# Summing squares at a layer's end: all eight on the vector engines instead of six, with two left to TensorE

## The chip, the cores and the metric

The kernel runs on one NeuronCore of a Trainium2 chip. The core has a matrix engine (TensorE, PE in the profile, with its weight loads shown as PEld), three engines for elementwise work (VectorE = DVE, ScalarE = ACT, GpSimd = POOL) and a queue that issues its transfers (SyncE = SP). Each engine takes its instructions strictly in the order of its own queue, and engines wait for each other through semaphores. The metric is the device time of one execution in microseconds; lower is better.

## The reference, cut to what matters

The computation is a two-layer encoder in float32 over two independent sequences, a prompt of 256 tokens and a sample of 512 tokens, with a model width of 1024. Layer 0 mixes tokens with an mLSTM, layer 1 with sliding-window attention; each layer ends in a convolutional feed-forward block, and each block is entered through an RMS norm.

```python
def rmsnorm(x, g):
    xf = x.astype(jnp.float32)
    y = xf * lax.rsqrt(jnp.mean(xf * xf, axis=-1, keepdims=True) + EPS)
    return (y * g.astype(jnp.float32)).astype(x.dtype)

def trunk(x, c, ...):
    for l in range(DEPTH):                                   # DEPTH = 2
        sh1, sc1, g1, sh2, sc2, g2 = ...                     # modulation from c
        h = rmsnorm(x, norm_g[l, 0]) * (1 + sc1) + sh1
        y = mlstm_mixer(h, ...) if l % 2 == 0 else swa_mixer(h, ...)
        x = x + g1 * y
        h = rmsnorm(x, norm_g[l, 1]) * (1 + sc2) + sh2
        x = x + g2 * conv_ffn(h, ...)
    return rmsnorm(x, final_g)
```

What matters here is the norm that follows a layer's feed-forward block: after layer 0 it is the norm in front of layer 1's attention, after layer 1 it is the final norm that makes the output. For each token it needs the mean of 1024 squares.

## The kernel before, in words

Activations are kept transposed: channels lie on the 128 partitions, in eight chunks of 128 channels (`KC` = 8), and tokens lie along the free axis, 768 of them (prompt first, then sample). The mean over channels is therefore a sum over eight chunks and over 128 partitions. Products of the large matrices are done as three TensorE passes over a high and a low half of each operand (`whi`, `wlo`), so one output tile of 128 channels by 256 tokens of the down projection takes six matmuls.

The feed-forward block (`ffn`) runs over eleven parts of the hidden width. In the last part, `down` handles the tokens in three ranges of 256: the two halves of the sample (here called range 0 and range 1) and the prompt. For each range it makes eight tiles, one per chunk. After each tile `resid` (line 590, DVE) adds it to the residual stream, and `Norm.square` squares the new chunk on ACT (line 111) and adds the square to a running sum (line 115) as long as the chunk's number is below `KC - on_pe`. Layer 0's adds run on GpSimd, layer 1's on VectorE.

After the eight tiles of a range its norm is queued as a generator (`stages`), whose steps are emitted between later tiles. The first step sums what is left over the partitions by matmuls with a constant vector of 1/1024 (`inv`): one matmul per summand and per block of 128 tokens, so two per summand here; in the trace each such float32 matmul leaves two records. Then come `+ EPS` (line 152), a power of -0.5 on GpSimd (line 153), and a matmul with the identity (`kct`) that spreads the result over the partitions. With it `apply` follows: after layer 0 `modulated` (lines 549 to 552), which writes the input `zh`, `zl` of the attention's projections; after layer 1 `output` (lines 574 to 582), which scales by the final gain on DVE (line 581) and GpSimd (line 579) and sends the result out.

The prompt's norm after layer 1 is the very last (`final`) and is handled apart: all of its squares go straight to TensorE (line 129). In `on_pe` terms: 8 for that one, 2 for the five others.

The order of instructions on each engine is set when the program is built, by a scheduler that works with its own estimates; only some stretches are written out by hand. Tiles for the results of matmuls (`pa`) come from a pool of four, temporary tiles (`nt`) from a pool of eight.

Of the kernel before, what the change touches and what calls it, by code (L numbers as in the profile page):

```python
# [18 lines left out]
KC = D // P  # L19
# [5 lines left out]
RANGES = ((256, 512, 0), (512, 768, 0), PROMPT)  # L25
# [54 lines left out]
def col(t):  # L80

    return t + (GAP if t >= 256 else 0)
# [85 lines left out]
class Net:  # L168
# [1203 lines left out]
    def ffn(self, l, xt, pool, last_tile, apply, keep=None):  # L1372
# [68 lines left out]
        def down(p, g):  # L1441
            ws = (w for _, w in self.halves(u0 + 3 * p + 2))
            chunk = lambda w, i: [t[:, 512 * i : 512 * (i + 1)] for t in w]

            def tile(w, c, rng):
                s0, s1, _ = rng
                o = self.pa()[:, : s1 - s0]
                cs = slice(c % 4 * P, (c % 4 + 1) * P)
                for i in range(2):
                    wh, wl = chunk(w, i)  # L1450
                    gh, gl = (g[:, z, i, col(s0) : col(s0) + s1 - s0] for z in range(2))
                    self.mm(o, wh[:, cs], gh, i == 0, False)
                    self.mm(o, wh[:, cs], gl, False, False)
                    self.mm(o, wl[:, cs], gh, False, i == 1)
                self.resid(xt, o, l, 40, c, rng)

            if p < NPART - 1:
                for h, w in enumerate(ws):
                    for rng in SAMPLE, PROMPT:
                        for c in range(4 * h, 4 * h + 4):  # L1460
                            tile(w, c, rng)
                return
            ws = list(ws)
            for rng in RANGES:
                final = keep is None and rng is RANGES[-1]
                norm = Norm(
                    self, xt, rng, apply, KC if final else 2, final,
                    None if keep is not None else nc.vector, 0.0 if keep is None or rng is RANGES[-1] else 1.3,
                )
                for c in range(KC):  # L1470
                    tile(ws[c // 4], c, rng)
                    norm.square(c)
                    if final and c > 1:
                        norm.begin(c - 1)
                    self.tick(0.65)
                if keep is not None:
                    self.save_x(xt, keep, rng)
                self.start(rng, norm.stages())

        prev = None  # L1480
        for p in range(NPART):
            g = up(p)
            if prev is not None:
                down(*prev)
            prev = (p, g)
        down(*prev)


# [179 lines left out]
```

## Time and profile before

| What | Before |
|---|---|
| Median of 3 runs | 1844.58 us |
| Lowest, highest | 1842.21 us, 1845.0 us |
| Profiled execution, its time | 1843.78 us |
| Its span, first to last instruction | 1842.0 us |
| TensorE busy | 1793.2 us, 97% of the span |
| VectorE, ScalarE, GpSimd busy | 1367.0, 895.3, 488.0 us |
| Mean granted TensorE clock | 0.994 |

A row of the timeline gives the start in us from the span's start, the length in us of what is merged in the row, the engine, the line, the operation, what it writes and reads, the size, how many instructions it stands for, and in brackets how long the engine sat idle before and what ended that. A length includes the emptying of a pipeline, so successive rows overlap; the time that an instruction takes from its engine is read from one start to the next. A row of windows gives a stretch, its length, the busy time of each engine in it with the number of instructions, then the granted TensorE clock (1.00 is full), and the share and rate of the transfers.

### The profile page before, as it was taken

How to read it: one execution, taken by the hardware profiler on the slowest of the kernel's cores; microseconds unless marked ns; L12 is line 12 of the kernel's file. 1: busy time of each engine (PE TensorE's matmuls, PEld its weight loads, DVE VectorE, ACT ScalarE, POOL GpSimd, SP SyncE). 2: the span in 40 equal slices, each digit the busy share in tenths (PEclk: the TensorE clock that was granted, in tenths of full speed). 3: DMA queues.
4: the chain of work that ended last, by engine and by line, in shares of the span. 5: the costliest groups of instructions: out<-in, count | busy, mean ns of one | idle time of the engine just before them, and what ended most of it. 6: DMA issues, size and time to landing. Idle time of an engine off the chain costs nothing.

```text
span 1842.0 us, 28931 instructions
## 1 busy us (share of the span) xinstructions
PE 1793.2 (97%) x11290; PEld 1657.4 (90%) x11290; DVE 1367.0 (74%) x2101; ACT 895.3 (49%) x1815; POOL 488.0 (26%) x386
## 2 busy tenths in 40 slices
PE   6999999999999999999999999999999999999997
PEld 3987887889998999999999999889989999999997
DVE  4755676886689877777777757766898777777776
ACT  4443443354456444444444556765564444444443
POOL 1001001021024333333331313430144333333322
PEclk9999999999999999999999999999999999999999
DMA  8344566546312221222223321124122222222212
GB/s 330 119 145 134 172 195 221 164 138 219 101 46 74 76 61 66 69 69 69 69 69 93 104 83 50 53 94 129 50 86 69 69 69 69 69 69 70 69 35 69
DMA packets 64245, 184.48 MB, mean 100 GB/s; under 512 B 6167, under 2 KB 23831, under 8 KB 64108
## 3 DMA queue, kind: packets, MB, share of 16 engines
q1 hardware_dynamic: 64108, 182.63, 30.8%
q8 instruction: 89, 1.46, 0.3%
q14 instruction: 48, 0.39, 0.1%
HBM read 176.17 MB, written 6.43 MB: 99 GB/s over the span
## 4 chain that ended last, share of the span: by engine, by line
PE 86%; DVE 6%; DMA 3%; ACT 2%; issue 1%; POOL 1%; SPq 0%; POOLq 0%; ACTq 0%; DVEq 0%
PE ps L254 27%; PE pa L254 25%; PE ps L1169 10%; PE ps L1172 10%; PE ps L1170 10%; PE pa L1008 1%; DMA slab<-in_adaln_w_dram 1%; DMA raw<-in_w_dram 1%; DVE wlo L261 1%; DVE ada L506 1%; DVE slab L590 1%; DMA raw<-in_adaln_w_dram 0%; PE pa L1172 0%; PE pa L1169 0%; PE pa L1170 0%
## 5 line engine op out<-in xcount | busy, mean ns | idle before, releaser
L260 ACT CAST whi<-raw 128x1024 fp32r<-128x1024 f32 x237 | 247.9, 1048 | 350.4 <-PE pa L254 161.4
L261 DVE TENSOR_TENSOR wlo<-raw,whi 128x1024 fp32r<-128x1024 f32 x237 | 316.6, 1337 | 119.8 <-ACT whi L260 117.3
L254 PE MATMUL pa<-slab,whi 128*128 128x256 f32 (+1 forms) x1472 | 346.6, 331 | 3.2 <-DVE slab L590 3.2
L254 PEld LDWEIGHTS pa<-slab,whi 128*128 128x128 f32 x1472 | 252.7, 188 | 27.5 <-DVE slab L590 4.5
L590 DVE SCALAR_TENSOR_TENSOR slab<-pa,mod,slab 128x256 f32<-128x256 f32 (+1 forms) x368 | 211.2, 592 | 70.8 <-PE pa L254 70.5
L254 PE MATMUL pa<-slab,wlo 128*128 128x256 f32 (+1 forms) x736 | 233.9, 330 | 0.0
L254 PE MATMUL ps<-zh,whi 128*128 128x256 f32 (+1 forms) x560 | 189.0, 339 | 2.3 <-ACT whi L260 1.7
L254 PE MATMUL ps<-zh,wlo 128*128 128x256 f32 (+1 forms) x560 | 184.1, 330 | 2.0 <-DVE wlo L261 2.0
L254 PE MATMUL ps<-zl,whi 128*128 128x256 f32 (+1 forms) x560 | 185.1, 332 | 0.0
L1169 PE MATMUL ps<-zh,whi 128*128 128x384 f32 x504 | 172.3, 342 | 3.6 <-ACT nt L1240 1.8
L1170 PE MATMUL ps<-zl,whi 128*128 128x384 f32 x504 | 169.9, 337 | 0.8 <-DVE zl L1126 0.8
L1172 PE MATMUL ps<-zh,wlo 128*128 128x384 f32 x504 | 168.9, 335 | 0.0
L254 PEld LDWEIGHTS pa<-slab,wlo 128*128 128x128 f32 x736 | 138.5, 188 | 13.1 <-DVE wlo L261 0.4
L1205 POOL TENSOR_TENSOR raw<-raw,raw 128x512 f32<-128x512 f32 x40 | 52.2, 1305 | 330.8 <-DVE wlo L261 259.4
L254 PE MATMUL ps<-slab,whi 128*128 128x384 f32 x512 | 132.0, 339 | 0.9 <-DVE slab L261 0.5
L1402 POOL TENSOR_TENSOR slab<-slab 128x772 f32<-128x772 f32 x44 | 86.5, 1967 | 164.6 <-DVE slab L1390 152.7
L1389 DVE SCALAR_TENSOR_TENSOR slab<-slab,cstt,slab 128x771 f32<-128x771 f32 x88 | 103.6, 1179 | 26.6 <-ACT slab L1387 26.5
L254 PEld LDWEIGHTS ps<-zh,whi 128*128 128x128 f32 x560 | 107.4, 192 | 15.9 <-issue 4.4
L506 DVE SCALAR_TENSOR_TENSOR ada<-raw,silc,ada 128x1024 f32<-128x1024 f32 x84 | 110.6, 1354 | 14.9 <-DMA raw<-in_adaln_w_dram 14.8
L1202 POOL TENSOR_TENSOR raw<-raw 128x512 f32<-128x512 f32 x40 | 68.5, 1712 | 200.1 <-DMA raw<-in_w_dram 169.7
L254 PEld LDWEIGHTS ps<-zh,wlo 128*128 128x128 f32 x560 | 107.2, 192 | 12.2 <-DVE wlo L261 2.9
L254 PEld LDWEIGHTS ps<-zl,whi 128*128 128x128 f32 x560 | 107.4, 192 | 11.9 <-issue 3.4
(291 smaller groups left out, 4265.7 us busy)
## 6 DMA issues: line engine op xcount, KB each, us to landing
raw<-in_w_dram SPq DMA_DIRECT2D x208, 512.0 KB, 3.7
raw<-in_adaln_w_dram SPq DMA_DIRECT2D x84, 512.0 KB, 4.6
slab<-in_x_dram SPq DMA_DIRECT2D x12, 512.0 KB, 6.8
slab<-in_adaln_w_dram SPq DMA_DIRECT2D x12, 512.0 KB, 10.3
slab<-mrows SPq DMA_DIRECT2D x8, 384.0 KB, 5.3
xs<-slab SPq DMA_DIRECT2D x6, 512.0 KB, 3.6
bt<-brow SPq DMA_DIRECT2D x16, 192.0 KB, 3.0
slab<-xs SPq DMA_DIRECT2D x6, 512.0 KB, 6.9
```

Source lines behind the costliest of these rows:

```text
L254: self.nc.tensor.matmul(out, lhsT, rhs, start=start, stop=stop)
L260: nc.scalar.copy(hi, src)
L261: return nc.vector.tensor_tensor(lo, src, hi.bitcast(F32), ALU.subtract)
L506: stt(acc[:, s], row, w, acc[:, s], ALU.mult, ALU.add)
L590: self.nc.vector.scalar_tensor_tensor(x, o, self.mod[l][:, gc + c, q : q + 1], x, ALU.mult, ALU.add)
L1169: mm(o, wh[:, k], hi[k], start=start and k == 0, stop=False, skip_group_check=True)
L1170: mm(o, wh[:, k], lo[k], start=False, stop=False, skip_group_check=True)
L1172: mm(o, wl[:, k], hi[k], start=False, stop=k == 3, skip_group_check=True)
L1202: tt(q[2], q[2], q[3], ALU.add)
L1205: tt(q[0], q[2], q[0], ALU.subtract)
L1389: stt(y[:, 1:], u[:, :-1], w(0), y[:, 1:], ALU.mult, ALU.add)
L1402: nc.gpsimd.tensor_tensor(y, y, yrow[:, j], ALU.mult)
```

## The change

For the first two ranges at the end of each layer `on_pe` goes from 2 to 0. The condition in `square` then holds for all eight chunks, so the squares of chunks 6 and 7 are also added to the running sum (two more adds per range at line 115, on GpSimd in layer 0 and on VectorE in layer 1), and one summand is left for the matmuls with `inv` where there were three. The prompt's ranges keep what they had: 2 after layer 0, all 8 after layer 1.

```diff
             for rng in RANGES:
                 final = keep is None and rng is RANGES[-1]
                 norm = Norm(
-                    self, xt, rng, apply, KC if final else 2, final,
+                    self, xt, rng, apply, KC if final else 2 if rng is RANGES[-1] else 0, final,
                     None if keep is not None else nc.vector, 0.0 if keep is None or rng is RANGES[-1] else 1.3,
                 )
```

In the built program this takes 16 `inv` matmuls (32 records) away and adds four adds on GpSimd and four on VectorE. The order of the other instructions changes only around the two layer ends. The transfers are the same, in the same order.

## The prediction

> **What bounds the kernel now.** I read the page's busy times and its chain first, then the groups by shape, then the timeline of each engine over the two layer ends, and last windows of the granted clock.
>
> ```profile
> PE 1793.2 (97%) x11290; PEld 1657.4 (90%) x11290; DVE 1367.0 (74%) x2101; ACT 895.3 (49%) x1815; POOL 488.0 (26%) x386
> PE 86%; DVE 6%; DMA 3%; ACT 2%; issue 1%; POOL 1%; SPq 0%; POOLq 0%; ACTq 0%; DVEq 0%
> ```
>
> TensorE is busy for 97% of the span and is 86% of the chain. Work taken from it is worth its full time, but only where no new wait opens in its queue; a wait that opens is paid in full as well.
>
> ```profile
> L254 PE MATMUL pa<-inv,nt 128*128 128x2 f32 x188 | 25.6, 259 | 1.1 <-DVE nt L115 0.6 <-ACT nt L111 0.3 <-POOL nt L115 0.3
> L115 POOL TENSOR_TENSOR nt<-nt,nt 128x256 f32<-128x256 f32 x25 | 19.2, 769 | 29.6 <-ACT nt L111 28.2
> ```
>
> The first row holds all matmuls with `inv` but the final norm's, 188 records. The change removes 32 of them. Its 259 ns is a length with an overlapping tail, so I price by starts below.
>
> **The change part by part.** Layer 0's end, TensorE first, then GpSimd, then ScalarE:
>
> ```profile
> 1021.74 0.40 PE L254 MATMUL pa<-slab,whi 128*128 128x256 f32 x2
> 1021.97 0.28 PE L254 MATMUL pa<-slab,wlo 128*128 128x256 f32 x1
> 1022.51 1.50 PE L254 MATMUL pa<-inv,nt 128*128 128x2 f32 x12 [0.26 <-POOL nt L115]
> 1023.87 0.48 PE L254 MATMUL pa<-slab,whi 128*128 128x256 f32 x2
> ...
> 1033.88 0.95 PE L254 MATMUL pa<-inv,nt 128*128 128x2 f32 x8
> 1034.68 0.36 PE L254 MATMUL ps<-zl,whi 128*128 128x256 f32 x1
> ...
> 1035.12 0.40 PE L254 MATMUL pa<-slab,whi 128*128 128x256 f32 x2
> ```
> ```profile
> 1018.44 4.02 POOL L115 TENSOR_TENSOR nt<-nt,nt 128x256 f32<-128x256 f32 x5 [9.37 <-ACT nt L111]
> 1023.36 0.73 POOL L115 TENSOR_TENSOR nt<-nt,nt 128x256 f32<-128x256 f32 x1 [0.91 <-ACT nt L111]
> ```
> ```profile
> 1021.39 0.42 ACT L111 ACTIVATE nt<-slab 128x256 f32<-128x256 f32 x1 [0.29 <-DVE slab L590]
> ...
> 1022.87 0.42 ACT L111 ACTIVATE nt<-slab 128x256 f32<-128x256 f32 x1 [0.29 <-DVE slab L590]
> ...
> 1032.79 0.81 ACT L111 ACTIVATE nt<-slab 128x256 f32<-128x256 f32 x2 [0.34 <-DVE zl L552]
> ```
>
> *Saved on TensorE.* Eight records cost 1034.68 - 1033.88 = 0.80 us and twelve cost 1.36, so 0.10 to 0.11 each. Eight records fewer in each of four ranges are 32 x 0.10 to 0.11 = 3.2 to 3.6 us; with the upsets of the matmul behind each scattered group, some 4 us at most.
>
> *Range 0 of layer 0, +1.5.* The five adds start 1018.44 and end 1022.46, (4.02 - 0.74)/4 = 0.82 from one to the next, and TensorE already waits for the fifth: it starts `inv` at 1022.51, 0.05 later. The changed program leaves the group at the same place of TensorE's queue, behind range 1's second tile, which ends about 1022.09. On GpSimd the order becomes: chunk 6's add, range 1's first add, chunk 7's add. Chunk 6's add runs 1022.54 to 1023.28. Range 1's add cannot start before its square, the row at 1022.87, ends at 1023.29; it starts at 1023.36 as now and ends 1024.09. Chunk 7's add is queued behind it, though its square (1021.39) is long there, and runs 1024.13 to 1024.87. TensorE starts `inv` at 1024.92 and needs 0.44 for four records (price quoted below, 1821.86 to 1822.30), so it is free at 1025.36 where it was at 1023.87: +1.49. The empty stretch is 1022.09 to 1024.92, 2.8 us. Behind the waiting group stand range 1's other tiles; DVE's residual adds and range 0's power wait for them, so everything shifts alike. If GpSimd put chunk 7's add ahead, the shift would be 0.8; if the extra adds were hidden it would be -0.9. I take +1.5, from the rows' own times.
>
> *Range 1 of layer 0, +0.1.* Eight records go (-0.8); a prompt tile moves from ahead of the group to behind it, and the three projection matmuls now behind it (1034.68 to 1035.12) move ahead. The square of chunk 7 is the first of the two at 1032.79 and ends near 1033.20; its add would then end at 1034.0 and `inv` start at 1034.05, take 0.44, upset the next matmul by 0.09, and the moved tile costs 0.70: 1035.28 (before the shift of +1.5). Now the same work is done at 1035.12. I call it +0.1, between -0.8 (add hidden) and +0.3.
>
> Layer 1's end, TensorE, then DVE, then ScalarE:
>
> ```profile
> 1812.10 0.39 PE L254 MATMUL pa<-slab,whi 128*128 128x256 f32 x2
> 1812.45 0.28 PE L254 MATMUL pa<-inv,nt 128*128 128x2 f32 x2
> ...
> 1817.00 0.71 PE L254 MATMUL pa<-kct,nr 128*128 128x128 f32 x4 [0.22 <-POOL nr L153]
> 1817.46 0.48 PE L254 MATMUL pa<-slab,whi 128*128 128x256 f32 x2
> ...
> 1821.86 0.58 PE L254 MATMUL pa<-inv,nt 128*128 128x2 f32 x4 [0.62 <-DVE nt L115]
> 1822.30 0.48 PE L254 MATMUL pa<-slab,whi 128*128 128x256 f32 x2
> ...
> 1823.81 0.95 PE L254 MATMUL pa<-inv,nt 128*128 128x2 f32 x8
> 1824.62 0.59 PE L129 MATMUL pa<-inv,nt 128*128 128x2 f32 x4
> ```
> ```profile
> 1812.08 1.06 DVE L590 SCALAR_TENSOR_TENSOR slab<-pa,mod,slab 128x256 f32<-128x256 f32 x2
> ...
> 1818.15 1.66 DVE L581 SCALAR_TENSOR_TENSOR slab<-slab,cstt,pa 128x256 f32<-128x256 f32 x4
> ...
> 1821.30 0.41 DVE L115 TENSOR_TENSOR nt<-nt,nt 128x256 f32<-128x256 f32 x1
> ```
> ```profile
> 1812.59 0.42 ACT L111 ACTIVATE nt<-slab 128x256 f32<-128x256 f32 x1 [0.18 <-DVE slab L590]
> ...
> 1817.75 0.37 ACT L574 COPY nt<-pa 128x256 f32<-128x256 f32 x1
> ```
>
> Half a tile is 1812.45 - 1812.10 = 0.35, a tile 0.70.
>
> *Range 0 of layer 1, +0.3.* Now TensorE spreads the group over the next four tiles, so nothing waits. In the changed order the whole group stands behind range 1's first tile, at 1812.45. DVE has the two residual adds until about 1813.06, then chunk 6's add; chunk 7's square ends at 1812.59 + 0.42 = 1813.01, and its add, which needs the one before, ends about 1813.81. From DVE to TensorE the row at 1821.30 gives 1821.86 - 1821.71 = 0.15. So `inv` runs 1813.96 to 1814.40, four tiles and an upset of 0.09 take 2.91, and the spreading matmul `kct` starts at 1817.31 instead of 1817.00. The new gap is 1.5 us; the 0.22 that `kct` waits now is gone.
>
> *Range 1 of layer 1, +1.0.* From `kct`, done at 1817.77, TensorE makes four tiles until 1820.68 and then stands before `inv`, which needs the sum of all eight. DVE is late: `output` of range 0 puts five multiplications of line 581, 0.39 apart ((1.66 - 0.48)/3), ahead of chunk 6's residual add. They wait for the copy of line 574, which stands behind chunk 4's square: tile until 1817.31, residual add from 1817.51 for 0.48, square 0.42, copy 0.37, so 1818.86 with the steps between engines. They also stand behind chunk 5's residual add (tile until 1818.56, add from 1818.76, 0.40) and the add of chunk 4 (0.33), so they run 1819.49 to 1821.45. Behind them come three residual adds (0.40 each) and three adds of squares (0.33, or 0.41 when the next one needs it): 1823.81. `inv` runs 1823.96 to 1824.40, two prompt tiles follow until 1825.90. Now the same work is done at 1824.62: +1.28 for both ranges of this layer. The gap is 3.3 us; the waits of 0.62 here and one before it vanish. If DVE kept the multiplications back, the gap would fall to some 1.3 us and the layer to -0.7.
>
> *Sum of waits and work:* 1.5 + 0.1 + 1.3 = +2.9. It is paid in full: from layer 0's end TensorE is the chain, and what is late next is only itself.
>
> *The clock.* Gaps of this length have a second price here:
>
> ```profile
> 121.70:125.11 3.41, 1.53 (x7) 0.83 (x6) 3.41 (x7) 1.12 (x2) 0.00 (x0) 1.00 0.77 262
> 125.12:128.53 3.41, 3.41 (x10) 2.64 (x9) 3.41 (x6) 0.00 (x0) 0.00 (x0) 0.50 0.85 293
> ```
> ```profile
> 145.60:149.01 3.41, 1.77 (x16) 1.53 (x14) 2.09 (x4) 1.49 (x6) 2.50 (x2) 1.00 0.02 5
> 149.02:152.43 3.41, 2.98 (x23) 2.78 (x24) 2.80 (x7) 2.62 (x10) 0.00 (x0) 1.00 0.26 87
> 1056.96:1060.37 3.41, 1.22 (x4) 0.31 (x4) 3.32 (x6) 3.38 (x11) 0.00 (x0) 1.00 0.00 0
> 1060.37:1063.78 3.41, 3.41 (x17) 3.41 (x17) 3.31 (x9) 2.02 (x5) 0.00 (x0) 0.50 0.22 54
> 1063.78:1067.19 3.41, 3.41 (x31) 3.41 (x30) 1.96 (x3) 0.92 (x1) 0.00 (x0) 1.00 0.41 133
> ```
>
> The halved stretches fall on a common grid of 3.41 us. Where TensorE was busy 1.22 or 1.53 us of a stretch, the next ran at clock 0.50; after 1.77 us it did not. So some 1.9 us empty within one stretch is enough. The halved stretch passed 17 matmuls where the next passed 31: 14 x 0.118 = 1.65 us lost, if TensorE sets the pace in it. The gap of 2.8 us holds 1.9 in one stretch for (0.9 + 0.9 + 0.6)/3.41 = 0.7 of the positions of the grid, that of 3.3 us for (1.4 + 1.4 + 0.1)/3.41 = 0.85; the gap of 1.5 us for none. Each drop costs between 0 (all of it in waits on DVE that are there anyway) and 1.65; near the upper end, since both gaps are followed by dense tiles: 1.5.
>
> The Trainium skill, "TensorE: Matmul & The Clock Gate", Part 1, says that the clock falls after at least one idle window of about 3.4 us, and tells to avoid gaps above that. By that sentence alone neither gap would drop the clock and the sum would stay at +2.9; this trace differs, since 1.22 us of work in a stretch did not keep the clock up. The same section's window of 3413 ns and its two rates agree with the 3.41 and 0.50 here.
>
> *Total:* 2.9 + 2 x 1.5 = +5.9, so 1843.78 + 5.9 = 1849.7 for the profiled execution. That one lies 0.8 below the median of the three runs; against the median it is 1844.58 + 5.9 = 1850.5.
>
> **The rivals.**
> - *One clock drop only,* because the grid cuts the other gap in two: 2.9 + 1.5, 1849.0.
> - *Waits, but no drop,* because a stretch of 3.41 must be empty from end to end, which no gap of 3.3 us or less can fill: 2.9 alone, 1847.5. For it: 1.77 us of work was enough at 145.60. Against it: the two halved stretches. This is the rule of the skill's page above.
> - *It is faster:* the extra adds end before TensorE arrives, and the 32 records are a clear gain of 3.2 to 4: 1840.9. The place is the first group of layer 0. It decides if chunk 7's sum is there by 1022.5 + 1.0, that is 1.4 us earlier than by GpSimd's rows, and if DVE in layer 1 is likewise 1.3 us earlier. TensorE already waits 0.26 and 0.62 for these very adds, which speaks against it.
> - *Worse:* range 1 of layer 0 gets the c7 sum late as well and a third drop follows: about +9, 1853.5. For it: TensorE waits for DVE's `zl` in that stretch; against it: DVE is busy there, not stalled.
>
> **How the numbers follow.** Two drops 0.47 (1850.5), one 0.27 (1849.0), none 0.13 (1847.5), faster 0.05 (1840.9), worse 0.08 (1853.5). The time is that of two drops; its own range is 1849 to 1852. The range 1846.5 to 1853.0 takes in one drop and none, with about 1 us for the spread of the runs (1842.21 to 1845.0), and leaves out the faster and most of the worse case. 0.2%, or 3.7 us, is about what a measurement of this kernel can tell from no change: 1848.3 is the limit. Slower: 0.47 + 0.08 + 0.8 x 0.27 = 0.77; same: 0.13 + 0.05 = 0.18; faster 0.05.
>
> **What would show it.** In the changed profile: 156 records of `inv` at line 254; a wait of TensorE for line 115 on GpSimd of 2.5 us or more near 1022, and two for line 115 on DVE, about 1.5 us near 1814 plus the shift and 3 us near 1822 plus the shift; clock 0.50 for 3.41 us just after the first and the last of these. I am wrong if the waits are below 1 us, which would mean that the added sums come earlier than the rows' pitches say, or if the clock stays up after gaps of 2.8 and 3.3 us.

## The result, and the profile after

The changed kernel takes 1856.70 us (median of 6 runs, 1852.19 to 1858.62) where the kernel before takes 1844.79 us in the runs beside it (median of 6): 1.0063 times as long, 95% interval 1.0052 to 1.0074, or +11.9 us. The direction was forecast, the size was not: 1850.5 with a range up to 1853.0. The profiled execution took 1855.8 us, 12.0 above that of before.

The page's busy times and chain, then two groups by shape (busy time in us, mean ns, idle time before and what ended it):

```profile
span 1853.8 us, 28886 instructions
...
PE 1796.3 (97%) x11258; PEld 1660.0 (90%) x11258; DVE 1367.6 (74%) x2105; ACT 894.7 (48%) x1815; POOL 493.3 (27%) x390
...
PE 86%; DVE 7%; DMA 3%; ACT 2%; issue 1%; POOL 1%; SPq 0%; POOLq 0%; DVEq 0%; ACTq 0%
```
```profile
L115 POOL TENSOR_TENSOR nt<-nt,nt 128x256 f32<-128x256 f32 x29 | 24.1, 832 | 29.9 <-ACT nt L111 28.5
L254 PE MATMUL pa<-inv,nt 128*128 128x2 f32 x156 | 22.5, 268 | 9.4 <-DVE nt L115 5.0 <-POOL nt L115 4.1 <-ACT nt L111 0.3
```

The 32 records of `inv` are gone, yet TensorE is busy 3.1 us longer (1796.3 for 1793.2): fewer instructions, some of them at half clock. And the matmuls with `inv` now have 9.4 us of idle time ahead of them where they had 1.1, nearly all of it for the adds of line 115. The four sums, in TensorE's timeline:

```profile
1024.01 0.61 PE L254 MATMUL pa<-inv,nt 128*128 128x2 f32 x4 [2.57 <-POOL nt L115]
...
1034.89 0.39 PE L254 MATMUL ps<-zl,whi 128*128 128x256 f32 x1 [0.56 <-DVE zl L552]
...
1037.84 0.61 PE L254 MATMUL pa<-inv,nt 128*128 128x2 f32 x4 [1.54 <-POOL nt L115]
...
1820.72 0.61 PE L254 MATMUL pa<-inv,nt 128*128 128x2 f32 x4 [1.44 <-DVE nt L115]
...
1831.11 0.98 PE L254 MATMUL pa<-inv,nt 128*128 128x2 f32 x4 [3.57 <-DVE nt L115]
```

Three of these waits are followed by a clock of 0.50. In the windows below, laid on the grid of 3.41 us that this execution shows, the clock is the number behind the five engines' busy times:

```profile
1021.96:1025.37 3.41, 1.35 (x11) 1.36 (x12) 0.17 (x2) 0.42 (x1) 2.34 (x4) 1.00 0.33 111
1025.38:1028.79 3.41, 3.41 (x18) 3.41 (x17) 1.45 (x3) 1.04 (x3) 1.69 (x3) 0.50 0.18 64
...
1035.62:1039.03 3.41, 1.87 (x16) 1.67 (x15) 2.62 (x7) 1.12 (x3) 3.27 (x4) 1.00 0.06 15
1039.04:1042.45 3.41, 3.41 (x18) 3.41 (x18) 1.46 (x4) 1.67 (x3) 0.88 (x2) 0.51 0.10 34
1042.45:1045.86 3.41, 3.41 (x31) 3.41 (x31) 3.28 (x6) 1.82 (x5) 3.17 (x4) 1.00 0.66 186
1827.51:1830.92 3.41, 0.03 (x1) 0.00 (x0) 3.31 (x9) 1.22 (x3) 0.41 (x1) 1.00 0.72 244
1830.93:1834.34 3.41, 3.23 (x15) 3.26 (x16) 0.68 (x3) 0.14 (x1) 0.69 (x1) 0.50 0.10 35
1834.34:1837.75 3.41, 3.41 (x18) 3.41 (x18) 0.97 (x2) 1.34 (x4) 0.00 (x0) 0.50 0.00 0
1837.76:1841.17 3.41, 3.41 (x32) 3.41 (x32) 2.24 (x6) 1.01 (x3) 1.42 (x2) 1.00 0.11 36
```

A halved stretch makes 18 matmuls where a full one makes 31 or 32 (the one at 1830.93 makes 15, because the wait still reaches into it). There is one behind each wait of layer 0, and two in a row behind the second wait of layer 1.

With the same matmuls of both traces laid side by side (all but those with `inv`, in order, start against start), the 12.0 us by which the profiled executions differ fall as follows:

| Where | Shift gained there |
|---|---|
| From the start to layer 0's end | -0.8 us |
| Layer 0's end | +6.3 us: wait of range 0 1.4, halved stretch 1.5, range 1 3.4 |
| Near 1343 us, inside layer 1 | +1.1 us |
| Layer 1's end | +5.0 us |

The rest, 0.4 us, lies behind the last matmul and in rounding. The +1.1 us is not at a sum at all. One VectorE subtraction of line 1126, which takes 0.55 us elsewhere, took 1.64 us because a GpSimd operation had started just ahead of it:

```profile
1341.95 2.31 DVE L1126 TENSOR_TENSOR zl<-slab,zh 128x384 fp32r<-128x384 f32 x2
```
```profile
1342.56 1.28 POOL L1205 TENSOR_TENSOR raw<-raw,raw 128x512 f32<-128x512 f32 x1 [22.88 <-DVE zl L1126]
```

### The profile page after: what moved, and what is told of

Same layout as the page of the kernel before. It is cut to its first block, busy times and chain, and to the rows that moved or that the text cites. A ratio compares the mean times of both kernels' runs of the same rounds, so it can differ in the third digit from the quotient of the medians.

```text
span 1853.8 us, 28886 instructions
## 1 busy us (share of the span) xinstructions
PE 1796.3 (97%) x11258; PEld 1660.0 (90%) x11258; DVE 1367.6 (74%) x2105; ACT 894.7 (48%) x1815; POOL 493.3 (27%) x390
## 3 DMA queue, kind: packets, MB, share of 16 engines
q8 instruction: 88, 1.44, 0.3%
## 4 chain that ended last, share of the span: by engine, by line
PE 86%; DVE 7%; DMA 3%; ACT 2%; issue 1%; POOL 1%; SPq 0%; POOLq 0%; DVEq 0%; ACTq 0%
PE ps L254 27%; PE pa L254 25%; PE ps L1169 10%; PE ps L1172 10%; PE ps L1170 10%; PE pa L1008 1%; DMA slab<-in_adaln_w_dram 1%; DMA raw<-in_w_dram 1%; DVE wlo L261 1%; DVE slab L590 1%; DVE ada L506 1%; DMA raw<-in_adaln_w_dram 0%; PE pa L1170 0%; PE pa L1172 0%; PE pa L1169 0%
## 5 line engine op out<-in xcount | busy, mean ns | idle before, releaser
L254 PE MATMUL pa<-slab,whi 128*128 128x256 f32 (+1 forms) x1472 | 350.6, 334 | 2.8 <-DVE slab L590 2.4
L254 PEld LDWEIGHTS pa<-slab,whi 128*128 128x128 f32 x1472 | 256.8, 192 | 26.9 <-DVE slab L590 3.6
L254 PEld LDWEIGHTS pa<-slab,wlo 128*128 128x128 f32 x736 | 140.9, 192 | 13.1 <-DVE wlo L261 0.4
```

Of the source, the lines that this page charges most:

```text
L254: self.nc.tensor.matmul(out, lhsT, rhs, start=start, stop=stop)
```

## Experiments

Theory A: the whole loss is TensorE waiting at the four sums, and the clock behind these waits. The rivals say that the two layers don't add, that the clock plays no part, that the place of the adds or later norms decide, or that something apart from the waits does. Each kernel was timed in turns with the kernel before on the same chip. All ratios are to the kernel before. The edits are shown against the changed kernel, e4's against e1 and e14's against e6.

| Run | What it has | Median us, beside it before | Ratio, 95% interval |
|---|---|---|---|
| e1 | change in layer 0 only | 1850.42, 1844.52 | 1.0033, 1.0020 to 1.0046 |
| e2 | change in layer 1 only | 1851.73, 1844.52 | 1.0037, 1.0024 to 1.0051 |
| e3 | e2, its waits filled with matmuls | 1846.66, 1844.52 | 1.0010, 1.0000 to 1.0019 |
| e4 | e1, adds on VectorE | 1851.25, 1844.52 | 1.0035, 1.0024 to 1.0046 |
| e5 | layer 0, range 0 only | 1849.64, 1844.71 | 1.0025, 1.0016 to 1.0035 |
| e6 | layer 0, range 1 only | 1848.79, 1844.71 | 1.0023, 1.0014 to 1.0033 |
| e7 | whole change, sums placed later | 1839.97, 1844.71 | 0.9973, 0.9964 to 0.9982 |
| e8 | two summands | 1851.58, 1844.71 | 1.0041, 1.0026 to 1.0055 |
| e9 | before, places of e7 | 1845.90, 1845.78 | 0.9992, 0.9983 to 1.0002 |
| e10 | e7's place in layer 0 only | 1850.74, 1845.78 | 1.0028, 1.0017 to 1.0039 |
| e11 | e7's place in layer 1 only | 1847.58, 1845.78 | 1.0015, 1.0005 to 1.0024 |
| e12 | whole change, places between its own and e7's | 1835.91, 1845.78 | 0.9948, 0.9932 to 0.9963 |
| e13 | before, places of e12 | 1841.79, 1845.12 | 0.9984, 0.9973 to 0.9994 |
| e14 | e6, range 1's adds on VectorE | 1843.66, 1845.12 | 0.9997, 0.9988 to 1.0007 |

### The two layers apart, and the clock (e1 to e4)

e1, layer 0 alone:

```diff
-                    self, xt, rng, apply, KC if final else 2 if rng is RANGES[-1] else 0, final,
+                    self, xt, rng, apply, KC if final else 2 if rng is RANGES[-1] or keep is None else 0, final,
```

> The change in layer 0 alone. Theory A (new waits of TensorE for the sums, and a halved clock behind each): the profile of the changed kernel moves by 6.3 us over layer 0's end, so about +6 us against before (ratio 1.0034), with one wait of 2.6 us and one of 1.5 us on GpSimd's adds and two stretches of 3.41 us at clock 0.50 that the kernel before does not have. Rival B (the loss is not bound to the places of the sums, but comes from the shifted order of the whole layer): the two layers' shares do not add up to the 11.9 us of the full change.

e2, layer 1 alone:

```diff
-                    self, xt, rng, apply, KC if final else 2 if rng is RANGES[-1] else 0, final,
+                    self, xt, rng, apply, KC if final else 2 if rng is RANGES[-1] or keep is not None else 0, final,
```

> The change in layer 1 alone. Theory A: +5 us (the shift over layer 1's end in the changed kernel's profile), waits of 1.4 and 3.6 us on VectorE's adds, and 6.8 us at clock 0.50 behind the second. Rival B: another figure than what is left of 11.9 us beside layer 0 alone.

e3 is e2 with matmuls that nobody needs, written into the bank of the sum before the sum overwrites it; TensorE's order in this part of the program is written out by hand, so that they stand right ahead of the two groups:

```diff
+                if keep is None:
+                    order.enter_context(self.tc.manual_schedule(engines={mybir.EngineType.PE}))
...
+                        norm.filler = {256: 7, 512: 18}.get(rng[0], 0)
...
+            for _ in range(self.filler):
+                hi, _ = net.quarter(net.B11)
+                net.mm(pm[:, :H], hi[0][:, :P], hi[0], True, True)
```

> Layer 1 alone, with 7 and 18 idle matmuls of 384 columns put on TensorE right ahead of its two waits (1.2 and 3.1 us of work whose result is overwritten), all else in the same order. Theory A: the waits end at the same times, the clock stays at 1.00, and the loss falls from 5 to some 2 us, so about 3 us less than with layer 1 alone. Rival C (the halved clock costs nothing, since the tail is paced by VectorE): the same time as layer 1 alone, or longer by what the fillers add.

e4 is e1 with the adds of layer 0's first two ranges on VectorE:

```diff
-                    None if keep is not None else nc.vector, 0.0 if keep is None or rng is RANGES[-1] else 1.3,
+                    None if keep is not None and rng is RANGES[-1] else nc.vector, 0.0 if keep is None or rng is RANGES[-1] else 1.3,
```

> Layer 0 alone, with the squares of its first two ranges added on VectorE in place of GpSimd. Theory A, with the GpSimd adds as the late link (0.82 us apart at best, 1.9 and 1.5 us beside a busy VectorE): the first wait falls below 1 us, no drop follows it, and the loss of layer 0 alone falls from 6 to between 0 and 3 us. Rival D (it is the place of the group in TensorE's queue that costs, whoever adds): 4 to 7 us as with GpSimd.

e1 costs 5.9 us, as expected, and e2 7.2, more than the 5 I expected; together 13.1, against 11.9 for the change. The layers add, within the intervals, and layer 0's 5.9 is twice what my steps for it give (1.5 + 0.1 and one drop, 3.1). e3 costs 2.1 in place of 7.2: with the waits filled, the clock stays up through both groups of layer 1.

The groups and the fillers in e3's timeline (line 258 is the changed file's line for what was 254):

```profile
1812.08 1.40 PE L258 MATMUL pa<-yh 128*128 128x384 f32 x7
...
1813.68 0.61 PE L258 MATMUL pa<-inv,nt 128*128 128x2 f32 x4 [0.20 <-DVE nt L115]
...
1821.69 3.37 PE L258 MATMUL pa<-yh 128*128 128x384 f32 x18 [1.20 <-DVE slab L585]
...
1824.90 0.50 PE L258 MATMUL pa<-inv,nt 128*128 128x2 f32 x4
```

And one window over layer 1's end, of e2, then of e3:

```profile
1805.00:1834.00 29.00, 24.02 (x167) 23.64 (x165) 18.38 (x47) 11.95 (x29) 4.68 (x7) 0.82 0.11 37
```
```profile
1805.00:1834.00 29.00, 27.26 (x217) 26.61 (x215) 21.26 (x54) 12.92 (x32) 5.14 (x7) 1.00 0.15 51
```

Laid side by side with the kernel before, the first group comes no sooner in e3 than in e2, and the second 0.7 us sooner, behind a stretch that isn't halved; up to each of them TensorE is only kept busy. Over layer 1's end e2's profiled execution loses some 6 us and e3's some 2.5, and between the medians the difference is 5.1. So the halved clock is the larger part of layer 1's 7 us, 3.5 of them by the profiles and 5 by the medians: this is shown. Behind the second group e3's hand-written order also sets the prompt's sums otherwise than e2 does; no run separates that, but neither kernel waits there for more than 0.4 us ahead of the last spreading matmul. In e2's execution the wait of 1.44 us brought a halved stretch as well, which it did not in the changed kernel's.

e4 missed: I expected 0 to 3 us and got 6.7, which is in rival D's range. The range's sum was late there too (1.49 us of wait at range 0's sum, now for VectorE), and new waits came for what VectorE makes besides: 0.99 us for line 590's additions, 0.17 and 1.06 for `zl`, 0.42 for `zh`. In its profiled execution 3.4 of the loss stand at layer 0's end; 2.0 came before that place and 1.1 at the subtraction of line 1126, so the time alone says little about the place; e7 to e13 below move it.

### One range at a time (e5, e6, e14)

```diff
-                    self, xt, rng, apply, KC if final else 2 if rng is RANGES[-1] else 0, final,
+                    self, xt, rng, apply, KC if final else 0 if rng is RANGES[0] and keep is not None else 2, final,
```

> Only layer 0's range 0 has all its squares added (one summand); layer 0's range 1 and all of layer 1 are as before. Theory A (each range costs its own wait and its own halved stretch): the first wait of 2.57 us comes back (1.5 us more than the kernel before's at this place), one halved stretch behind it (1.5 us), less some 0.4 us of matmuls: +2.5 to +3 us on the kernel before. Rival E (range 0 makes range 1's adds late too, whoever adds them): +4 to +6, with a second wait on range 1's sum.

e6 has the same line with `RANGES[1]`:

> Only layer 0's range 1 has all its squares added. Theory A (GpSimd's adds of range 1 are drawn out by VectorE's work beside them, whatever range 0 does): two or more adds of range 1 take over 1 us, TensorE waits 1 to 2 us for the sum and has a halved stretch behind it: +2.5 to +3.5. Rival F (they are late only because range 0's later norm moves VectorE's work onto them): the adds take 0.73 us, no wait over 0.3 us, +0 to +0.3, as the prediction had it.

e5 shows the wait of 2.57 us at the sum of range 0 again and no later wait on a sum. Its profiled execution (1847.46 us, the shortest of nine) has no halved stretch there, because the grid's edge fell into the gap:

```profile
1020.52:1023.93 3.41, 1.85 (x16) 1.65 (x14) 1.70 (x4) 1.67 (x4) 3.05 (x5) 1.00 0.95 334
1023.94:1027.35 3.41, 2.41 (x20) 2.41 (x21) 0.88 (x3) 0.37 (x1) 1.66 (x3) 1.00 0.01 3
```

The same gap, 1022.37 to 1024.94, is cut in 1.6 and 1.0 us. The median, 4.9 us above before's, is more than the 2.5 to 3 I gave it; it is in the range of rival E, but that rival's wait on range 1's sum is not there.

e6 costs 4.1 us, a little more than theory A's 2.5 to 3.5: range 1 alone is late, whatever range 0 does, so rival F falls. Its wait of 1.54 us has two halved stretches behind it, where e1 and the changed kernel have one. e5 and e6 do not add up to e1 (4.9 and 4.1 against 5.9); the intervals allow for the difference. GpSimd's three adds and VectorE's work beside them, in e6:

```profile
1032.89 4.34 POOL L115 TENSOR_TENSOR nt<-nt,nt 128x256 f32<-128x256 f32 x3 [2.99 <-ACT nt L111]
```
```profile
1032.93 1.27 DVE L552 SCALAR_TENSOR_TENSOR zl<-nt,mod,zh 128x256 fp32r<-128x256 f32 x3
1034.12 0.47 DVE L549 SCALAR_TENSOR_TENSOR nt<-slab,gain,pa 128x256 f32<-128x256 f32 x1
1034.51 0.48 DVE L590 SCALAR_TENSOR_TENSOR slab<-pa,mod,slab 128x256 f32<-128x256 f32 x1
1034.90 1.74 DVE L552 SCALAR_TENSOR_TENSOR zl<-nt,mod,zh 128x256 fp32r<-128x256 f32 x3
```

Three adds that take 0.73 us each alone took 4.34. The first started 0.04 ahead of three subtractions of line 552 and lasted 1.9: the 1.19 us that those occupy (1032.93 to 1034.12) plus its own 0.73 are 1.92. During the second add the next three subtractions took 1.74 where the first three took 1.27. So the two engines take turns, and what they share is held by operations that read two tiles from the ordinary on-chip memory (`nt` and `zh`, `nt` and `nt`); the rows between, which read one operand from `pa`, let the add run. The subtraction at 1343 us (`slab` and `zh`) is the same thing the other way round. The Trainium skill, "GPSIMD Engine Reference", Section 8 (Key points), says that GpSimd shares its memory interfaces with VectorE and contends with VectorE instructions that have two such inputs; this trace agrees, with 1.9 us for 0.73.

e14 makes range 1's adds on VectorE in e6:

```diff
-                    None if keep is not None else nc.vector, 0.0 if keep is None or rng is RANGES[-1] else 1.3,
+                    None if keep is not None and rng is not RANGES[1] else nc.vector, 0.0 if keep is None or rng is RANGES[-1] else 1.3,
```

> As e6_l0_range1 (only layer 0's range 1 has all its squares added), with that range's adds on VectorE in place of GpSimd; range 0's stay on GpSimd. Theory A (range 1's sum is late because GpSimd's adds are drawn out beside VectorE): no add over 0.6 us, the wait for the sum falls from 1.5 us to under 0.8, no halved stretch: 1844 to 1846.5. Rival L (the sum is late because VectorE is the engine behind at this place, and adds on it are queued as well): a wait of 1 us or more for the sum or for zl: 1847 to 1850.

The time, 1843.66, is what theory A gave, but the trace doesn't give it the credit. The wait for the sum is gone. In its place TensorE waits 0.99 us for line 590 and 1.06 and 0.17 for `zl`, 0.43 for `zh`, and there is a halved stretch as before: at 1058 us the matmuls stand 3.8 us behind before's, against 4.7 in e6. Rival L has the mechanism. What saves e14 is another place, the very end of layer 0. There the kernel before has a wait and a halved stretch of its own:

```profile
1060.17 0.43 PE L254 MATMUL pa<-zl,whi 128*128 128x256 f32 x1 [2.18 <-DVE zl L552]
```
```profile
1057.00:1075.00 18.00, 15.82 (x113) 14.90 (x114) 15.96 (x29) 12.38 (x29) 0.00 (x0) 0.91 0.31 97
```

The same window in e14:

```profile
1057.00:1075.00 18.00, 18.00 (x143) 16.88 (x142) 17.56 (x32) 15.03 (x33) 0.00 (x0) 1.00 0.28 85
```

There e14 gains some 4 us. The changed kernel keeps that wait and that stretch (its shift stays at +5.5 from 1040 to 1075). What removes them in e14 was not isolated.

### How many summands (e8)

```diff
-                    self, xt, rng, apply, KC if final else 2 if rng is RANGES[-1] else 0, final,
+                    self, xt, rng, apply, KC if final else 2 if rng is RANGES[-1] else 1, final,
```

> The first two ranges of both layers are added up to chunk 6, and chunk 7's square stays a summand of its own: two summands in place of three (before) or one (changed). Theory A (the loss is the last adds in the chain after the last square): the four waits fall by one add each, to about 1.5, 0.8, 1.0 and 2.5 us, and with them one or two of the three halved stretches: 1847 to 1851. Rival H (the place of the loss is the add of chunk 6 behind a slow engine, not of chunk 7): 1854 to 1857, as the whole change.

The waits were 1.04, 0.76, 0.91 and 2.92 us. The three shorter ones left the clock at 1.00; the last, over a stretch with 0.5 us of work or less, was followed by two halved stretches. The time, 1851.58, is just above what theory A gave and below rival H's: with one add fewer in the chain no halved stretch is left at the first three sums, but those at the fourth, which is the dear one, stay.

### The same change, later in the queue (e7, e9 to e13)

The last argument of `Norm` is the planner's time between the end of a range and the place of its sum. e7:

```diff
-                    None if keep is not None else nc.vector, 0.0 if keep is None or rng is RANGES[-1] else 1.3,
+                    None if keep is not None else nc.vector, 0.0 if final else 3.9 if keep is None else 1.3 if rng is RANGES[-1] and False else 0.0 if rng is RANGES[-1] else 5.2,
```

(The branch with `and False` is never taken: the prompt's ranges keep 0.0.)

> The changed kernel with the matmuls of each changed sum placed later: 3 to 4 tiles more of other work ahead of them (5.2 in place of 1.3 in layer 0, 3.9 in place of 0 in layer 1, in the planner's microseconds). Theory A (the whole loss is TensorE waiting at these sums and the clock behind the waits): no wait over 0.5 us at the four sums, no halved stretch there, and the saved matmuls show: 1841 to 1845. Rival G (norms that come later only move the wait to the tiles that need their results, or past the end): 1848 to 1857, with new waits on zl, zh or the final output.

1839.97: 16.7 us under the changed kernel and 4.7 under the kernel before, and 1 us under theory A's range. The four sums start without a wait on line 115. Rival G's waits on `zl` came, in two pieces of 1.06 and 1.24 us, and two halved stretches stand behind the shorter one, against theory A; but they are outweighed. In the trace its first sum starts some 4.6 us later than before's, with seven tiles more of 0.7 us ahead of it, and the three others have six more, so my "3 to 4 tiles" was too low. e9 puts the three summands of before at the same places:

> The kernel before (three summands), with the same later places as the run e7_later (5.2 in place of 1.3 in layer 0, 3.9 in place of 0 in layer 1). Theory A (the later place pays only because it hides the longer sum; the gain of e7_later is the saved matmuls and the wait of 0.6 us): within 2 us of the kernel before, 1843 to 1846.5, and 2 to 5 us above e7_later. Rival G (the later place pays by itself, for any number of summands): 1839 to 1841.5, as e7_later, so that the change is worth nothing.

It takes what before takes, within its interval. So this later place by itself brings nothing that shows; it pays by hiding the longer sum. e10 and e11 split it by layer (5.2 in layer 0 and 0 in layer 1; 1.3 and 3.9):

> The changed kernel with the later place in layer 0 alone (5.2 in place of 1.3); layer 1 as in the change. Theory A: layer 0's 6 us go and its saved matmuls show, layer 1's 7 us stay: 1846 to 1851, that is 6 to 9 us under the changed kernel. Rival J (the later place helps in one layer only, and it is layer 1): 1854 to 1858.

> The changed kernel with the later place in layer 1 alone (3.9 in place of 0); layer 0 as in the change. Theory A: layer 1's 7 us go and its saved matmuls show, layer 0's 6 us stay: 1846 to 1850. Rival K (the later place helps in layer 0 only): 1854 to 1858.

e10 lies 0.0035 of the time under the changed kernel's ratio (6.5 us), e11 0.0048 (8.9 us), both within what theory A gave; together 15.3 of e7's 16.6. Rivals J and K fall. e12 takes a part of it back, 3.9 in layer 0 and 2.6 in layer 1 (its two sums of layer 0 have five tiles more ahead of them than before's, those of layer 1 four more; the first starts some 3 us later), and e13 does so for the kernel before:

```diff
-                    None if keep is not None else nc.vector, 0.0 if keep is None or rng is RANGES[-1] else 1.3,
+                    None if keep is not None else nc.vector, 0.0 if rng is RANGES[-1] else 2.6 if keep is None else 3.9,
```

> As e7_later, with one tile less of other work ahead of each sum (3.9 in layer 0, 2.6 in layer 1). Theory A (what counts is that the place covers the sum): the first three sums are still covered or nearly so, layer 1's range 1 (3.6 us of wait in the changed kernel) keeps 0 to 1.5 us of wait: 1839 to 1845. If the cover is lost at one sum and the clock falls behind it: 1845 to 1849.

> The kernel before (three summands) with the places of e12_less_later (3.9 in layer 0, 2.6 in layer 1). Theory A (the change itself brings the gain as soon as its sums are covered): as the kernel before or up to 3 us faster, 1842 to 1846, so 6 to 10 us above e12_less_later. Rival G (the place brings it, whatever the number of summands): 1835 to 1838.

e12 is the fastest of all, 1835.91 (four runs), 9.9 us under the kernel before and 3 under the range that I gave it. Its sums are covered, none waits for line 115, and both layer ends run at full clock but for the last four matmuls of the program. All that TensorE waits for between 1016 and 1075 us, and the window there:

```profile
PE pa L254 <- DVE slab L590: 1.1, 1, 1.1
```
```profile
1016.00:1075.00 59.00, 57.81 (x478) 56.55 (x477) 48.67 (x100) 36.12 (x81) 16.25 (x22) 1.00 0.37 118
```

The changed kernel makes 376 matmuls in that window at a mean clock of 0.91, the kernel before 445 at 0.97. e13 gains 3.3 of the 9.9 us without the change (ratio 0.9984, a shade below theory A's range), so the change brings the rest, 0.0036 or 6.6 us; between e7 and e9 it brings 0.0019 or 3.5 us. Taken from the runs' intervals as independent, these are uncertain by some 3.4 and 2.4 us. The saving that I worked out, 3.2 to 3.6 us of matmuls, fits both, and that one is larger than the other is not shown. In e12's profiled execution 5.6 us are gained at layer 0's end, where the wait on `zl` near 1060 is gone, and 3.5 at layer 1's. e13 lost the wait near 1060 too, but waits 0.9 us for a sum (the prompt's, at 1043.28) that e12 does not, in an execution that was the longest of its nine. That short wait, with few wide matmuls beside it in the stretch, has a halved stretch behind it:

```profile
1041.27:1044.68 3.41, 2.49 (x21) 2.10 (x19) 3.41 (x7) 1.31 (x4) 1.95 (x2) 1.00 0.66 197
1044.69:1048.10 3.41, 3.41 (x17) 3.41 (x17) 3.41 (x10) 3.10 (x8) 0.71 (x1) 0.50 0.29 113
```

## Why the prediction was right and where it was wrong

*Range 0 of layer 0, +1.5:* right, with its reason. The wait was 2.57 us for GpSimd, the shift +1.42, and the halved stretch behind it brought +1.53 where I took 1.5.

*Range 1 of layer 0, +0.1:* this step failed, and it is 3.3 of the 6.1 us that are missing. I gave chunk 7's add 0.74 us after its square. The three adds there, which I priced at 0.74 each at most, took 4.35 us together (1.92, 1.48 and 0.91), beside the same subtractions of line 552 as in e6:

```profile
1034.31 4.35 POOL L115 TENSOR_TENSOR nt<-nt,nt 128x256 f32<-128x256 f32 x3 [3.31 <-ACT nt L111]
```
```profile
L115 POOL TENSOR_TENSOR nt<-nt,nt x29: 721/731/1921, 6.8 to 1045.3; 128x256 f32<-128x256 f32 x29
```

(the second is the group with its shortest, median and longest duration in ns). TensorE waited 1.54 for the sum and 0.56 and 0.17 for `zl`, and a third drop followed. This was my last rival, "worse", with a chance of 0.08. I counted VectorE being "busy there, not stalled" against it. That is what speaks for it: a busy VectorE, with operations that read two tiles from ordinary memory, is what holds GpSimd up there. And e14 shows that the adds are no cheaper on VectorE at that place, since VectorE is itself late there.

*Range 0 of layer 1, +0.3:* measured +0.32, with a wait of 1.44 for my 1.5.

*Range 1 of layer 1, +1.0:* right in place and reason, and short by some 0.5 us. The five multiplications of line 581 do stand ahead of the residual additions. The gap was 3.57 us of idle time for my 3.3, and the sum's matmul started at 1831.11, which without the shift of 6.67 that layer 1's end began with is 1824.44, for my 1823.96:

```profile
1826.55 2.04 DVE L581 SCALAR_TENSOR_TENSOR slab<-slab,cstt,pa 128x256 f32<-128x256 f32 x5
...
1830.02 0.94 DVE L115 TENSOR_TENSOR nt<-nt,nt 128x256 f32<-128x256 f32 x2
```

*The clock, 2 x 1.5:* both places are right, and so is the cost of one stretch, but there were four halved stretches for my two: one at layer 0's range 1, and a second one in a row behind the long gap of layer 1. I took from two examples that a drop lasts one stretch; the same trace also has one of two stretches, near 40 us. For layer 1 I had 1.3 of waits and 1.5 of clock and it cost 5.0; the 2.2 between are the 0.5 above and some 1.7 for the second stretch. They are the next part of the missing 6.1. The +1.1 at 1343 us is in no step, and the -0.8 before layer 0's end goes against it.

The rule of the Trainium skill, "TensorE: Matmul & The Clock Gate", Part 1, that the clock falls after an idle window of about 3.4 us, holds for the gap of layer 1, whose stretch held 0.03 us of work. It does not hold for the two of layer 0, where 1.35 and 1.87 us of work in a stretch did not keep the clock up. My own limit, some 1.9 us empty, isn't the measure either: 1.54 us empty was enough ahead of 1039.04, 0.92 in e13, and in e5 1.56 was not.

What sorts the stretches at the two layer ends is how many columns of matmuls began in them. I counted them in all sixteen traces, from 1000 to 1080 us and from 1790 us to the last matmul; a wide matmul has 256 columns (the second number of its size in a row), one with `inv` only 2, and some 29 wide ones fit into a stretch. At full clock, 33 of the 34 stretches that were followed by 0.50 had at most the worth of 11 wide matmuls, and 509 of the 510 that were followed by 1.00 had 11 or more. At half clock, all 11 that were followed by another at 0.50 had 12 or less, and all 25 after which the clock came back had more than 12. The stretch ahead of 1039.04 has 10, e13's above has 4 in spite of 2.49 us of busy time, e5's at 1020.52 has 14; and the halved one at 1830.93, into which the wait still reached, has 11, so that a second followed. Earlier in the traces, where matmuls of other shapes run, this count doesn't sort them: in e5 and e6 the clock fell near 140 us behind 18 and 16.

The saving on TensorE fits what was measured (3.5 us between e7 and e9), and the rival "it is faster" fell only because the sums came late: with the place moved, in e7 and e12, it is what happens.

## What to carry to other kernels

Work taken off the bounding engine and put into a chain that it waits for must be paid with distance in its queue: the change lost 11.9 us where its sums stood and gained 9.9 us together with a place some 3 us later (the place without the change gained 3.3), so move the consumer in the same edit. Price an operation at the place where it will run, beside what runs there, not by its mean elsewhere; for GpSimd next to a VectorE that reads two tiles from ordinary memory that was up to 2.6 times its length alone. And count a gap on TensorE with the clock behind it, which can cost as much as the gap: waits of 0.9 to 1.5 us had a halved stretch behind them in some runs and none in others, and the count of wide matmuls that are left in the stretch of 3.41 us told which, at these layer ends.

## What was not expected of the hardware

- One GpSimd add of 128x256 took 0.73 us alone and 1.9 beside VectorE operations with two inputs from ordinary memory, which is their time added to its own; in the other direction a VectorE subtraction went from 0.55 to 1.64 us.
- The halved clock lasted 3.41 us behind some gaps and 6.83 us behind others. Emptier stretches ahead do not sort them: 0.03 us of work was followed by two halved stretches, but before's 1.22 us and after's 1.35 and 1.87 by one each, while in e6 and e7 two followed on gaps of about 1 to 1.5 us. The matmuls in the halved stretch itself do, at the layer ends: with 12 wide ones or fewer another halved stretch followed (11 cases), with more none did (25 cases).
- Busy time did not keep the clock up. In e9 TensorE was busy for all 3.41 us of the stretch from 1823.36, but with only 9 wide matmuls among the 29 that began in it, and the clock was 0.50 in the next; about 11 wide ones were the limit at the layer ends. What the limit is for other shapes stays open.
- Matmuls that nobody needs, put into a wait of TensorE, kept its clock at 1.00 and took 5 us off the median (e3 against e2; 3.5 us between the two profiled executions).
